# Moving the softmax transposes of the odd attention heads into another pair of PSUM banks

## The chip, the core and the metric

The kernel runs on one core of a Trainium2 chip. The metric is the device time of one execution in microseconds (us). Of TensorE's clock the profile gives the share that was granted; full speed is 2.4 GHz.

The names of the engines in the rows are those of the profile: PE is TensorE's matmul, PEld its weight load, DVE is VectorE, ACT is ScalarE, POOL is GpSimd, SP is the engine whose queue starts the transfers.

## What is computed

Two layers of an encoder over 256 tokens of width 1024. Each layer is a half-step feed-forward block, a mixing block, and another half-step feed-forward block. The mixing block is where the change lies:

```
h = rms_norm(x);  z = h @ w_in            # q, k, v of two attentions, and two gates
o_sw = sliding_window_gqa(...)            # 8 heads of 64, 2 key heads, a learned sink per head
o_na = neighbourhood_attention(...)       # 8 heads of 64
merged = g_A * (o_na @ P_A) + g_B * (o_sw @ P_B);   x = x + merged @ w_out
```

Each attention head computes scores of 256 queries against 256 keys, adds a bias, takes a softmax over the keys and multiplies by the values.

## The kernel before

The 256 tokens are two tiles of 128 rows (T = 2). A float32 matmul is done as three matmuls of split operands (`three`, L166 to L169): every weight piece that arrives by DMA is split into a high part by ACT (L181) and a low part by DVE (L182), and the two parts sit in rings of six (`RING`). PE thus runs a nearly unbroken stream of 512-column matmuls.

The mixing block (`mix`) projects in an order that is written out by hand in the string `ORDER`: Q and K are the queries and keys of the sliding window, q, k, v those of the neighbourhood attention, g the gates. Between the projections, tokens `a4`, `a5` and so on start the next head: first the 8 heads of the sliding window (`sw`), then the 8 of the neighbourhood (`na`). A head passes through three functions, which the kernel puts off by a count of matmuls (`defer`, `tick`, with the lags `P_LAG` and `V_LAG`):

- `front` (L522 to L550): four score matmuls into a PSUM tile `sc` (L536), DVE adds the bias and takes the row extremum (L539), ACT the exponential (L542), DVE the reciprocal of the row sum (L548), POOL scales the rows, which are then the softmax rows `S` (L549).
- `turn` (L553 to L561): PE transposes the 256 x 256 rows in four 128 x 128 pieces into one PSUM bank, the tile `pt` (L557). ACT copies it out as the high part `ph` (L181), DVE then computes the low part `pl` from `pt` and `ph` (L182). The bank is free again when both have read it.
- `back` (L564 to L580): the transposed rows times the values into the PSUM tile `po` (L571), then out by ACT and DVE (L575, L576).

The eight PSUM banks are given out by pools: `ps_g` has two for the projections (tag `g`), `ps_acc` has one for `pt`, one for `po` and two for `sc`, and `ps_tp` has two (tag `tp`) for all other transposes. In the mixing block those are the turns of the queries (L480), the turns of the keys (L497) and the merging of the two branches (L696). A turn of the keys of the neighbourhood uses both `tp` banks at once, four heads in each. ACT copies a bank out as `kh` (L499), and DVE then computes `kl` from the bank and `kh` (L500).

PE's order is the order in which the program issues (it is scheduled by hand); the orders of ACT, DVE and POOL are set when the kernel is built, by a planner that simulates the engines. All three functions of a head have raised priority there.

In the text below, a head is named by its attention and its number from 0: sw h3 is the fourth head of the sliding window. The transposes of the 16 heads of a layer run on PE in the order sw h0 to h7, na h0 to h7.

Of the kernel before, what the change touches and what calls it, by code (L numbers as in the profile page):

```python
# [11 lines left out]
F32 = mybir.dt.float32  # L12
# [9 lines left out]
P = 128  # L22
# [4 lines left out]
T = S // P  # L27
# [28 lines left out]
def hybrid_encoder(ctx, tc, x, w_gu1, w_d1, w_in, b_gate, qk_gain, rpb, sink, t5,  # L56
# [8 lines left out]
    ps_acc = ctx.enter_context(tc.tile_pool(name="ps_acc", bufs=1, space=PSUM))  # L65
    ps_tp = ctx.enter_context(tc.tile_pool(name="ps_tp", bufs=2, space=PSUM))
# [85 lines left out]
    def defer(lag, key, fn):  # L152
        later.append((now[0] + lag, len(later), key, fn))
        later.sort(key=lambda e: e[0])

    def need(*keys):
        for e in [e for e in later if e[2] in keys]:
            later.remove(e)
            e[3]()
# [16 lines left out]
    def flipped(ap):  # L176
        step, n = ap.ap[-1]
        return bass.AP(tensor=ap.tensor, offset=ap.offset + step * (n - 1), ap=[*ap.ap[:-1], [-step, n]])

    def split_to(hi, lo, src):  # L180
        linked("act", lambda: nc.scalar.activation(hi, src, AF.Copy))  # L181
        linked("dve", lambda: nc.vector.tensor_tensor(lo, src, hi.bitcast(F32), ALU.subtract))  # L182
# [272 lines left out]
    def mix(l, n, after):  # L455
        with tc.tile_pool(name="mix", bufs=1) as mp:
# [52 lines left out]
            def attend(name, ins, qT, kh, kl, kidx, bias_of, vcol, ready, oT, sink_l=None):  # L509
                oh, ol = oT  # L510
                po = [None, None]
                with tc.issue_after(rstd_done[0].ins):
                    bias = [bias_of(0), bias_of(1)]

                def urgent(fn):
                    def run(*args):
                        with tc.high_priority(500):
                            fn(*args)
                    return run

                @urgent
                def front(h):  # L522
                    need(*ins)
                    if h + 2 < NH:
                        bias.append(bias_of(h + 2))
                    b = bias.pop(0)
                    least = FMAX
                    if sink_l is not None:
                        sk, least = (v[:, sink_l * NH + h:sink_l * NH + h + 1] for v in (snk, nsnk))
                    ps = ps_acc.tile([P, T, S], F32, name="sc", tag="sc", bufs=2)  # L530
                    S_ = mp.tile([P, T, S], F32, name="S", tag="S", bufs=LAG)
                    mx = small.tile([P, T], F32, name="mx", tag="mx")
                    sm = small.tile([P, T], F32, name="sm", tag="sm")
                    for t in range(T):
                        for i, k in enumerate((kh, kl)):
                            nc.tensor.matmul(ps[:, t, :], qT[:, h, t * P:(t + 1) * P], k[:, kidx(h), :],  # L536
                                             start=i == 0, stop=i == 1)
                    for t in range(T):
                        nc.vector.tensor_tensor_reduce(S_[:, t, :], ps[:, t, :], b(t), -1.0, least,  # L539
                                                       ALU.add, ALU.min, mx[:, t:t + 1])  # L540
                    for t in range(T):
                        nc.scalar.activation(S_[:, t, :], S_[:, t, :], AF.Exp, bias=mx[:, t:t + 1], scale=-1.0,  # L542
                                             accum_out=sm[:, t:t + 1])
                    if sink_l is not None:
                        es = small.tile([P, T], F32, name="es", tag="es")
                        nc.scalar.activation(es, mx, AF.Exp, bias=sk)
                        nc.vector.tensor_tensor(sm, sm, es, ALU.add)
                    nc.vector.reciprocal(sm, sm)  # L548
                    nc.gpsimd.tensor_tensor(S_, S_, sm.unsqueeze(2).to_broadcast([P, T, S]), ALU.mult)  # L549
                    defer(P_LAG, (name, h, 0), lambda: turn(h, S_))  # L550

                @urgent
                def turn(h, S_):  # L553
                    tp = ps_acc.tile([P, T, T, P], F32, name="pt", tag="pt")
                    for t in range(T):
                        for kt in range(T):
                            nc.tensor.transpose(tp[:, kt, t, :], S_[:, t, kt * P:(kt + 1) * P], ident)  # L557
                    ph = mp.tile([P, T, T, P], F32R, name="ph", tag="ph", bufs=2)
                    pl = mp.tile([P, T, T, P], F32R, name="pl", tag="pl", bufs=2)
                    split_to(ph, pl, tp)  # L560
                    defer(V_LAG, (name, h, 1), lambda: back(h, ph, pl))  # L561

                @urgent
                def back(h, ph, pl):  # L564
                    assert ready()
                    if h % 2 == 0:
                        po[0] = ps_acc.tile([P, 2, T, P], F32, name="po", tag="po")
                        po[1] = mp.tile([P, T, P], F32, name="o", tag="o", bufs=2)
                    for kt in range(T):
                        for i, p in enumerate((ph, pl)):  # L570
                            nc.tensor.matmul(po[0][:, h % 2], vcol(kt, h), p[:, kt], start=kt + i == 0,  # L571
                                             stop=kt + i == 2)
                    a, b = (0, DH) if h % 2 == 0 else (DH, 0)
                    o, ov = po[1], flipped(po[0][:, h % 2])
                    nc.scalar.activation(o[a:a + DH], ov[b:b + DH], AF.Copy)  # L575
                    nc.vector.tensor_tensor(o[a:a + DH], o[a:a + DH], ov[a:a + DH], ALU.add)  # L576
                    if h % 2:
                        split_to(oh[:, h // 2], ol[:, h // 2], o)

                for h in range(NH):  # L580
                    yield lambda h=h: front(h)
# [79 lines left out]
            for token in ORDER.split():  # L661
                if token[0] == "a":
                    it, h = next(heads)
# [149 lines left out]
```

## Time and profile before

| | |
|---|---|
| median of 3 runs | 1094.89 us (1094.21 to 1095.57) |
| the profiled execution | 1094.91 us, of it a span of 1093.1 us |
| PE busy | 1079.0 us (99%) |
| DVE busy | 855.3 us (78%) |
| ACT busy | 659.2 us (60%) |
| POOL busy | 116.2 us (11%) |
| granted TensorE clock | 1.000 |

The span goes from the first to the last instruction. PE has matmuls in flight in 99% of it; matmuls overlap in the pipeline, so the start of one against the start of the next says more than the busy time. A 512-column matmul starts some 0.23 us after the one before it, though each is shown as 0.39 us long.

### The profile page before, as it was taken

The numbers are of one execution on the slowest core, as the hardware profiler recorded it, in microseconds if no ns is written. First come the engines' busy times: TensorE is split into PE (matmuls) and PEld (weight loads), VectorE is DVE, ScalarE is ACT, GpSimd is POOL, SyncE is SP. The second block draws the span as 40 slices with busy tenths as digits, with TensorE's granted clock in tenths as the row PEclk, the third lists the DMA queues.
The fourth block names the chain that finished last, engine by engine and source line by source line (L and its number), as shares of the span: only waits on it lengthen the run. The fifth ranks groups of instructions, "written<-read, shape, count | busy, mean of one in ns | idle before, by whom it ended". The sixth has DMA issues, their size and how long they took to land.

```text
span 1093.1 us, 14659 instructions
## 1 busy us (share of the span) xinstructions
PE 1079.0 (99%) x5137; PEld 889.3 (81%) x5137; DVE 855.3 (78%) x1298; ACT 659.2 (60%) x1002; POOL 116.2 (11%) x118
## 2 busy tenths in 40 slices
PE   9999999999999999999999999999999999999998
PEld 7888878888888888887888888788888888888877
DVE  6887778889886778776877786787888767878676
ACT  6665544788764566554465665457877546656442
POOL 1400000243510000000000000003534000000000
PEclk9999999999999999999999999999999999999999
DMA  7876556765654666654757665557666555776553
GB/s 239 267 222 210 185 169 206 232 189 154 192 176 136 209 213 214 210 194 149 245 175 227 215 217 168 189 161 236 185 186 182 177 168 162 226 234 202 183 174 105
DMA packets 98827, 212.62 MB, mean 195 GB/s; under 512 B 7569, under 2 KB 13745, under 8 KB 98753
## 3 DMA queue, kind: packets, MB, share of 16 engines
q1 hardware_dynamic: 98560, 211.60, 61.5%
q8 instruction: 40, 0.66, 0.2%
q0 software_dynamic: 192, 0.08, 0.1%
q14 instruction: 35, 0.28, 0.1%
HBM read 210.59 MB, written 1.06 MB: 194 GB/s over the span
## 4 chain that ended last, share of the span: by engine, by line
PE 78%; DVE 10%; DMA 6%; issue 3%; ACT 3%; DVEq 0%; ACTq 0%
PE g L168 19%; PE g L169 19%; PE g L167 19%; DMA raw<-in_w_d 4%; DVE wl L182 4%; PE acc L167 4%; PE acc L168 4%; PE acc L169 4%; PE tp L314 2%; ACT wh L181 2%; PE tp L198 1%; DVE v L343 1%; PE g L234 1%; PE pt L557 1%; PE sc L536 1%
## 5 line engine op out<-in xcount | busy, mean ns | idle before, releaser
L182 DVE TENSOR_TENSOR wl<-raw,wh 128x1024 fp32r<-128x1024 f32 (+1 forms) x340 | 408.1, 1215 | 66.8 <-ACT wh L181 65.2
L181 ACT ACTIVATE wh<-raw 128x1024 fp32r<-128x1024 f32 (+1 forms) x340 | 349.8, 1045 | 158.6 <-DMA raw<-in_w_d 41.0
L167 PE MATMUL g<-wh,xh 128*128 128x512 f32 (+1 forms) x976 | 389.9, 399 | 0.0
L169 PE MATMUL g<-wh,xl 128*128 128x512 f32 (+1 forms) x976 | 379.0, 388 | 0.0
L168 PE MATMUL g<-wl,xh 128*128 128x512 f32 (+1 forms) x976 | 377.4, 387 | 0.4 <-DVE wl L182 0.4
L169 PEld LDWEIGHTS g<-wh,xl 128*128 128x128 f32 x976 | 183.3, 188 | 40.4 <-DVE xl L182 1.1
L168 PEld LDWEIGHTS g<-wl,xh 128*128 128x128 f32 x976 | 184.0, 189 | 32.1 <-DVE wl L182 0.8
L167 PEld LDWEIGHTS g<-wh,xh 128*128 128x128 f32 x976 | 183.5, 188 | 30.8 <-DVE hh L435 0.2
L433 ACT ACTIVATE sg<-g,rs_y 128x256 f32<-128x256 f32 x88 | 41.5, 471 | 135.3 <-PE g L169 133.8
L343 DVE TENSOR_TENSOR u<-raw 128x512 f32<-128x512 f32 x56 | 38.8, 693 | 79.5 <-DMA raw<-in_w_d 79.2
L167 PE MATMUL acc<-wh,hi 128*128 128x512 f32 x200 | 78.9, 395 | 0.0
L169 PE MATMUL acc<-wh,lo 128*128 128x512 f32 x200 | 78.0, 390 | 0.0
L168 PE MATMUL acc<-wl,hi 128*128 128x512 f32 x200 | 77.9, 389 | 0.0
L173 POOL TENSOR_TENSOR rs_y<-ms,mhalf 128x1 f32<-128x1 f32 x12 | 7.2, 602 | 659.5 <-DVE ms L219 652.5
L435 DVE SCALAR_TENSOR_TENSOR hh<-g,rs_y,sg 128x256 f32<-128x256 f32 x88 | 42.1, 479 | 38.2 <-ACT sg L433 38.0
L549 POOL TENSOR_TENSOR S<-S,sm 128x512 f32<-128x512 f32 x32 | 37.1, 1161 | 71.4 <-DVE sm L548 45.2
L169 PEld LDWEIGHTS acc<-wh,lo 128*128 128x128 f32 x200 | 37.5, 188 | 8.1
L168 PEld LDWEIGHTS acc<-wl,hi 128*128 128x128 f32 x200 | 37.6, 188 | 7.7
L167 PEld LDWEIGHTS acc<-wh,hi 128*128 128x128 f32 x200 | 37.6, 188 | 7.6
L542 ACT ACTIVATE S<-S,mx 128x256 f32<-128x256 f32 x64 | 31.8, 498 | 7.5 <-DVE mx L539 7.4
L314 PEld LDWEIGHTS tp<-ident,hh 128*128 128x128 f32 x176 | 24.5, 140 | 11.7 <-DVE hh L435 0.6
L314 PE MATMUL tp<-ident,hh 128*128 128x128 f32 x176 | 33.4, 272 | 0.0
(190 smaller groups left out, 1460.0 us busy)
## 6 DMA issues: line engine op xcount, KB each, us to landing
raw<-in_w_gu SPq DMA_DIRECT2D x176, 512.0 KB, 4.4
raw<-in_w_d SPq DMA_DIRECT2D x100, 512.0 KB, 4.4
raw<-in_w_in SPq DMA_DIRECT2D x64, 512.0 KB, 4.6
raw<-in_w_out SPq DMA_DIRECT2D x16, 512.0 KB, 3.5
bb<-in_b_gate SPq DMA_DIRECT2D x16, 256.0 KB, 3.7
raw<-in_w_bsw SPq DMA_DIRECT2D x8, 512.0 KB, 4.4
raw<-in_w_bna SPq DMA_DIRECT2D x8, 512.0 KB, 3.5
raw<-in_w_d SPq DMA_DIRECT2D x12, 256.0 KB, 3.6
```

The source lines that it names most:

```text
L167: nc.tensor.matmul(ps, xh, wh, start=first, stop=False)
L168: nc.tensor.matmul(ps, xh, wl, start=False, stop=False)
L169: nc.tensor.matmul(ps, xl, wh, start=False, stop=last)
L181: linked("act", lambda: nc.scalar.activation(hi, src, AF.Copy))
L182: linked("dve", lambda: nc.vector.tensor_tensor(lo, src, hi.bitcast(F32), ALU.subtract))
L198: nc.tensor.transpose(tp[:, i, :], xs[t][:, k * P:(k + 1) * P], ident)
L314: nc.tensor.transpose(tp[:, SLOT[t][i], :], hh[:, i * P:(i + 1) * P], ident)
L343: sub = lambda to, x, y: nc.vector.tensor_tensor(to, x, y, ALU.subtract)
L433: nc.scalar.activation(sg, ps[:, :FC], AF.Silu, scale=rstd[t])
L435: nc.vector.scalar_tensor_tensor(hh, ps[:, FC:], rstd[t], sg, op0=ALU.mult, op1=ALU.mult)
L542: nc.scalar.activation(S_[:, t, :], S_[:, t, :], AF.Exp, bias=mx[:, t:t + 1], scale=-1.0, accum_out=sm[:, t:t + 1])
L549: nc.gpsimd.tensor_tensor(S_, S_, sm.unsqueeze(2).to_broadcast([P, T, S]), ALU.mult)
```

## The change

The transposes of the odd heads take their PSUM tile from the pool `ps_tp`, tag `tp`, in place of `ps_acc`, tag `pt`. Exempt is head 1 of the sliding window (the only attention with `sink_l`), so it is sw h3, h5, h7 and na h1, h3, h5, h7: seven of the sixteen heads of each layer. The other nine stay in the bank `pt`. The sizes, the four transposes of a head and their order on PE, the copies and their engines stay as they are.

```
                 @urgent
                 def turn(h, S_):
-                    tp = ps_acc.tile([P, T, T, P], F32, name="pt", tag="pt")
+                    if h % 2 and (sink_l is None or h > 1):
+                        tp = ps_tp.tile([P, T, T, P], F32, name="pt", tag="tp")
+                    else:
+                        tp = ps_acc.tile([P, T, T, P], F32, name="pt", tag="pt")
                     for t in range(T):
                         for kt in range(T):
                             nc.tensor.transpose(tp[:, kt, t, :], S_[:, t, kt * P:(kt + 1) * P], ident)
```

## Rows read from the trace of the kernel before

**Rows 1.** The page, part 1: busy time of each engine, share of the span, instructions.

```profile
PE 1079.0 (99%) x5137; PEld 889.3 (81%) x5137; DVE 855.3 (78%) x1298; ACT 659.2 (60%) x1002; POOL 116.2 (11%) x118
```

**Rows 2.** Who PE waited for, over the whole span: microseconds in all, times, longest.

```profile
...
PE pt L557 <- DVE sm L548: 2.1, 2, 1.0
PE pt L557 <- DVE pl L182: 1.7, 2, 0.9
...
PE g L168 <- DVE wl L182: 0.4, 1, 0.4
```

**Rows 3.** The timeline of PE in the first layer, around the transposes of sw h3 (256.49) and sw h4 (261.63): start, length, line, what is written from what, count; in brackets the idle time before and what ended it.

```profile
256.25 0.39 PE L169 MATMUL g<-wh,xl 128*128 128x512 f32 x1
256.49 0.60 PE L557 MATMUL pt<-ident,S 128*128 128x128 f32 x4
...
260.39 0.39 PE L169 MATMUL g<-wh,xl 128*128 128x512 f32 x1
261.63 0.63 PE L557 MATMUL pt<-ident,S 128*128 128x128 f32 x4 [0.85 <-DVE pl L182]
```

**Rows 4.** The timeline of DVE there: the low part of sw h2 (253.98), the work up to the two low parts of the keys, the low part of sw h3 (260.81), and the next idle time of DVE.

```profile
253.98 0.68 DVE L182 TENSOR_TENSOR pl<-pt,ph 128x512 fp32r<-128x512 f32 x1
...
256.82 1.21 DVE L182 TENSOR_TENSOR wl<-raw,wh 128x1024 fp32r<-128x1024 f32 x1
257.94 0.75 DVE L500 SCALAR_TENSOR_TENSOR kl<-tp,qkg,kh 128x512 fp32r<-128x512 f32 x1
...
257.94 1.41 DVE L500 SCALAR_TENSOR_TENSOR kl<-tp,qkg,kh 128x512 fp32r<-128x512 f32 x2
...
260.81 0.68 DVE L182 TENSOR_TENSOR pl<-pt,ph 128x512 fp32r<-128x512 f32 x1
...
263.00 0.75 DVE L623 SCALAR_TENSOR_TENSOR gate<-g,rs_y,bb 128x512 f32<-128x512 f32 x1 [0.92 <-PE g L169]
```

**Rows 5.** The last use of the `tp` banks by others before sw h3, on PE and on ACT, and the rows of sw h4 on POOL (timelines of the three engines).

```profile
253.55 1.03 PE L497 MATMUL tp<-ident,kn 128*128 128x128 f32 x8
...
255.87 1.26 ACT L499 ACTIVATE kh<-tp,qkg 128x512 fp32r<-128x512 f32 x2
...
257.08 1.85 POOL L549 TENSOR_TENSOR S<-S,sm 128x512 f32<-128x512 f32 x1 [4.10 <-PE pt L557]
```

**Rows 6.** The timeline of PE in the first layer around the transposes of na h3 (298.95), na h4 (304.50) and na h5 (308.70).

```profile
298.59 0.40 PE L169 MATMUL g<-wh,xl 128*128 128x512 f32 x1
298.95 0.52 PE L557 MATMUL pt<-ident,S 128*128 128x128 f32 x3
...
303.18 0.28 PE L571 MATMUL po<-pl,va 128*128 128x256 f32 x1
304.50 0.52 PE L557 MATMUL pt<-ident,S 128*128 128x128 f32 x3 [1.05 <-DVE sm L548]
...
307.52 0.28 PE L571 MATMUL po<-ph,va 128*128 128x256 f32 x1
...
308.70 0.60 PE L557 MATMUL pt<-ident,S 128*128 128x128 f32 x4
```

**Rows 7.** The timelines of DVE and POOL there: the low parts of na h2 (298.11) and na h3 (303.68), the reciprocal of na h5 (304.28), the output of na h2 (305.47), and the scaled rows of na h4 and na h5.

```profile
298.11 0.69 DVE L182 TENSOR_TENSOR pl<-pt,ph 128x512 fp32r<-128x512 f32 x1
...
303.68 0.68 DVE L182 TENSOR_TENSOR pl<-pt,ph 128x512 fp32r<-128x512 f32 x1
304.28 0.15 DVE L548 RECIPROCAL sm<-sm 128x2 f32<-128x2 f32 x1
...
305.47 0.40 DVE L576 TENSOR_TENSOR o<-o,po 64x256 f32<-64x256 f32 x1
...
297.77 1.04 POOL L549 TENSOR_TENSOR S<-S,sm 128x512 f32<-128x512 f32 x1 [1.39 <-DVE sm L548]
...
304.57 1.88 POOL L549 TENSOR_TENSOR S<-S,sm 128x512 f32<-128x512 f32 x1 [2.89 <-DVE sm L548]
```

**Rows 8.** Busy time of the engines in that stretch, 295 to 307 us (number of instructions in brackets), granted clock, share and rate of the transfers.

```profile
295.00:307.00 12.00, 10.95 (x62) 9.16 (x61) 10.66 (x22) 9.14 (x20) 6.18 (x4) 1.00 0.60 184
```

**Rows 9.** The same places in the second layer: PE at sw h3 (797.58), sw h4 (802.73), na h3 (840.19), na h4 (845.75), and the first low part of the keys on DVE.

```profile
797.58 0.60 PE L557 MATMUL pt<-ident,S 128*128 128x128 f32 x4
...
801.49 0.39 PE L169 MATMUL g<-wh,xl 128*128 128x512 f32 x1
802.73 0.52 PE L557 MATMUL pt<-ident,S 128*128 128x128 f32 x3 [0.85 <-DVE pl L182]
...
839.68 0.40 PE L169 MATMUL g<-wh,xl 128*128 128x512 f32 x1
840.19 0.63 PE L557 MATMUL pt<-ident,S 128*128 128x128 f32 x4
...
844.46 0.28 PE L571 MATMUL po<-pl,va 128*128 128x256 f32 x1
845.75 0.41 PE L557 MATMUL pt<-ident,S 128*128 128x128 f32 x2 [1.01 <-DVE sm L548]
...
799.04 0.74 DVE L500 SCALAR_TENSOR_TENSOR kl<-tp,qkg,kh 128x512 fp32r<-128x512 f32 x1
```

**Rows 10.** Two of the first lines of PE in the kernel (timeline): five matmuls of 512 columns without data, and the first transposes behind them.

```profile
4.66 2.48 PE L117 MATMUL idle<-blank 128*128 128x512 f32 x5
6.94 0.66 PE L198 MATMUL tp<-ident,x 128*128 128x128 f32 x4
```

## The prediction

> **What bounds the kernel now.** The page's busy times come first [rows 1]: PE is busy in 99% of the span, DVE in 78%, ACT in 60%. So only time in which PE stands still can be won, and any new standstill of PE is paid in full. The second view is who PE waited for [rows 2]. The entries for `pt` make 3.8 us in four waits, all in the mixing blocks; a wait for a split weight (`wl`) occurs once, for 0.4 us, so the weights come early enough. The third view is the timeline of PE at those waits, read by starts, since idle time counted from modelled ends comes out too small. A transpose starts 0.24 us after the 512-column matmul ahead of it (256.25 to 256.49) [rows 3]. sw h4 starts at 261.63, where 260.39 + 0.24 = 260.63 was due: 1.00 us lost. na h3: 298.95 against 298.83, 0.12. na h4: 304.50 against 303.18 + 0.12 (a 256-column matmul is half as long) = 303.30, 1.20 [rows 6]. In the second layer the same heads lose 802.73 - 801.73 = 1.00, 840.19 - 839.92 = 0.27 and 845.75 - 844.58 = 1.17 [rows 9]. Together 2.32 + 2.44 = **4.76 us**.
>
> What each waited for shows on DVE: the low part `pl` of the head before. sw h3's ends at 260.81 + 0.68 = 261.49, and sw h4 starts 0.14 later [rows 3, 4]; na h2's ends at 298.80 and na h3 starts 0.15 later; na h3's ends at 304.36 and na h4 starts 0.14 later [rows 6, 7]. The view of waits names a reciprocal (`sm`) for na h4, because one ends at 304.43; but that is na h5's, which na h4 does not read, and the constant 0.14 points to `pl`. So these are waits for the one bank `pt`.
>
> **The change, part by part.** No instruction is added, removed or reordered on PE, no transfer changes, and no queue is moved past. Only the bank that seven heads wait for is another.
>
> *Waits removed.* After the change sw h4 follows sw h2 in `pt`, whose low part ends at 254.66, and its own rows are scaled at 257.08 + 1.85 = 258.93 [rows 4, 5]: nothing holds it at 260.63. na h3 goes to `tp`, which by then only earlier odd heads have used. na h4 follows na h2 (298.80), with its rows scaled at 298.81 [rows 7]. The two waits of that stretch go as well. Gain **4.76 us**, if nothing else is late next.
>
> *A wait added.* The two `tp` banks are not idle when sw h3 comes. PE fills both with the keys of the second token tile at 253.55, 2.94 us ahead of it; ACT reads the first from 255.87 on, and DVE reads it last: `kl` of the first four heads runs 257.94 to 258.69, behind a weight split of 1.21 us [rows 4, 5]. sw h3 starts at 256.49 now; it would have to start at 258.69 + 0.14 = 258.83, **2.34 us later**. In the second layer `kl` ends at 799.78, so 799.92 against 797.58, again 2.34 [rows 9]. All of PE queues behind it: the scores of sw h5, the gate projection, and sw h4. Nothing that decides when `kl` runs comes after sw h3 on PE, so I see no reason for another place of `kl` in DVE's queue.
>
> Bounds of this term, for each layer. Below: if the planner put `kl` right behind its `kh` (first half of 1.26 us, so about 256.50), it would end at 257.25 and leave 257.39 - 256.49 = 0.90; nothing would be left if ACT too took the keys ahead of its weight split. Above: if the bank given is that of the second four heads, whose `kl` ends at 257.94 + 1.41 = 259.35, it is 3.00; with one more split of 1.21 us ahead, 3.55. I take 2.34, the order that the trace shows in both layers.
>
> A page of the Trainium skill, "Perfetto Trace Analysis", section "Optimizing Tensor Performance" (Matmuls), says that independent groups should rotate through different PSUM banks so that the evacuation of one overlaps the next. By that rule alone the 4.76 us would be the result; the rows of the keys say that the other banks are in use at the one place that matters.
>
> *The other odd heads* find `tp` free: sw h5 comes behind sw h4, which is not before 261.63, and the keys' second bank is free at 259.35 [rows 3, 4]; later ones each have a bank of which the head four before was the last user. na h5, at 308.70, needs its rows, scaled at 306.45, 2.25 us early [rows 6, 7].
>
> *What is late next.* After sw h4 PE is 2.34 - 1.00 = 1.34 us behind the trace of before. DVE stands idle for 0.92 us at 263.00 waiting for PE [rows 4], so it can follow. At na h3 and na h4 PE gets 0.12 and 1.20 back and is level again.
>
> *The sum.* First layer 2.34 - 2.32 = +0.02, second 2.34 - 2.44 = -0.10; together **-0.08 us**. The profiled execution took 1094.91 us (span 1093.1 and 1.8 around it), practically the median of 1094.89. Forecast **1094.8 us**: no change. What a measurement of this kernel can tell from no change is some 0.2%, 2.2 us.
>
> **The rivals.**
>
> *A. The keys are out of the way (faster).* The planner, which simulates the banks too, gives `kl` and `kh` earlier places, so that sw h3 does not wait: 1094.91 - 4.76 = 1090.15 us. If only `kl` moves, behind its `kh`, 0.90 us are left in each layer: 1094.91 - 4.76 + 1.80 = 1091.95. For it: both instructions are ready before they run, since the keys' transposes are done 1.3 us ahead of `kh` and a split of 1.21 us runs ahead of `kl` though it is not urgent. Against it: the same order stands in both layers, and nothing ahead of it changes.
>
> *B. The saved waits return at `back` of na h3 (slower).* DVE is busy in 10.66 of the 12 us from 295 to 307 [rows 8]. Without the wait of na h4, PE comes to `back` of na h3 as early as it does now, at 307.52, though all before it ran 1.34 us late [rows 6]. `back` writes the bank that DVE reads for the output of na h2 until 305.87 [rows 7]. With the usual 0.14 us the wait begins once that read ends after 307.38, 1.5 us later than now; a slip of DVE by the whole 1.34 us just does not reach it, so DVE's order would have to get worse too. The price is at most what was saved there, 1.32 and 1.44 us in the two layers: 1094.83 + 2.76 = 1097.6.
>
> *C. The clock falls in the long wait (slower).* The longest idle time of PE behind a first matmul is now 1.05 us [rows 6], and the clock stays granted in full through it (1.00) [rows 8]; 2.34 us are not in the trace. At the start of the kernel, before PE had worked for long, five 512-column matmuls took 6.94 - 4.66 = 2.28 us [rows 10], where later 5 x 0.23 = 1.15 do: the lower of the two levels, 1.2 against 2.4 GHz. One such stretch in each layer adds 2 x 1.13 = 2.3 us: 1097.1 or more.
>
> "TensorE: Matmul & The Clock Gate" in the Trainium skill, Part 1, says that the slow clock is the state at rest and that activity lifts it; no run shown so far has an idle time as long as the one forecast.
>
> **How the numbers follow.** The forecast gets 0.55: all its terms are read at one place and recur in both layers. A gets 0.25, since the order of two instructions decides it. B gets 0.14, C 0.06. The forecast's own range is 1092.9 (a `kl` about 1 us earlier) to 1096.2 (2 x 0.66, the second bank). The range for 8 in 10 reaches down over A to 1090.0 and up to B's price, 1097.6; it leaves out the far end of C, splits that slip twice, and gains above 4.9 us. Faster by over 0.2% is A, 0.25; slower by over 0.2% is B and C, 0.20; within it, 0.55.
>
> **What would show it.** In the changed profile PE should start the transposes of sw h3 some 0.14 us after the first `kl`, with an idle time of about 2 us in front, in both layers, and `tp` or `kl` should appear among what PE waited for. sw h4, na h3 and na h4 should start 0.24 and 0.12 us after the matmul ahead of them; later users of `tp` should show no wait. The forecast is wrong if sw h3 starts without that idle time (A), if `po` shows a wait at na h3 (B), or if matmuls behind sw h3 start 0.45 us apart (C).

## The result, and the profile after

The changed kernel took 1096.95 us in the median (1094.15 to 1098.66 over 20 runs), the kernel before 1094.91 us; the ratio is 1.0019, with a 95% interval of 1.0012 to 1.0025. It is slower by 2.0 us, and its runs spread over 4.5 us (those before over 1.6 us, without one run of 3409.17 us, which the ratio leaves out). The mean granted clock differs from run to run: 0.997 in eight of the 20 runs (1097.8 us on average), 0.998 in nine (1096.7 us), 0.999 or 1.000 in three (1094.8 us); the kernel before has 0.999 or 1.000 in every run of the experiments below. In the profiled run, 1095.51 us with a span of 1093.7 us, it is 0.998.

Who PE waited for in the changed kernel, over the whole span (microseconds, times, longest):

```profile
PE pt L560 <- DVE kl L500: 4.4, 2, 2.2
PE idle L117 <- DVE blank L112: 1.7, 1, 1.7
PE g L168 <- DVE cl L182: 1.6, 4, 0.8
PE tp L198 <- DVE x L299: 1.3, 3, 0.4
PE sc L536 <- DVE skT L500: 0.6, 2, 0.3
PE g L168 <- DVE wl L182: 0.4, 1, 0.4
```

The four waits of `pt` [rows 2] are gone, and two waits for the keys' low part `kl` have come. Rows 2 leave out the largest entry of that view before the change:

```profile
PE g L168 <- DVE cl L182: 2.5, 6, 0.9
```

`cl` is the low part of a weight of the feed-forward blocks; after the change it is 1.6 us in four waits. They lie outside the mixing blocks in both kernels. The other entries stand as they were. (`turn` now has its transposes in line 560, `back` its matmuls in line 574.)

The timeline of PE in the first layer: sw h3 at 258.46, sw h4 at 262.63, na h3 at 299.79, na h4 at 304.15; below it DVE's first `kl`:

```profile
255.87 0.39 PE L169 MATMUL g<-wh,xl 128*128 128x512 f32 x1
258.46 0.63 PE L560 MATMUL pt<-ident,S 128*128 128x128 f32 x4 [2.20 <-DVE kl L500]
...
262.39 0.39 PE L169 MATMUL g<-wh,xl 128*128 128x512 f32 x1
262.63 0.60 PE L560 MATMUL pt<-ident,S 128*128 128x128 f32 x4
...
299.56 0.39 PE L169 MATMUL g<-wh,xl 128*128 128x512 f32 x1
299.79 0.60 PE L560 MATMUL pt<-ident,S 128*128 128x128 f32 x4
...
304.03 0.28 PE L574 MATMUL po<-pl,va 128*128 128x256 f32 x1
304.15 0.60 PE L560 MATMUL pt<-ident,S 128*128 128x128 f32 x4
...
257.56 0.74 DVE L500 SCALAR_TENSOR_TENSOR kl<-tp,qkg,kh 128x512 fp32r<-128x512 f32 x1
```

sw h3 was due at 255.87 + 0.24 = 256.11 and comes at 258.46, 2.35 us late and 0.16 us after `kl` ends at 258.30 (before: no wait [rows 3]). sw h4 follows its matmul by 0.24 us, na h3 by 0.23, na h4 by 0.12: the waits of [rows 3, 6] are gone.

In the second layer the same wait has a sequel. The timeline of PE there, and below it the busy times and the granted clock (the column after POOL) in the stretch behind sw h3 of either layer:

```profile
796.50 0.39 PE L169 MATMUL g<-wh,xl 128*128 128x512 f32 x1
799.09 0.63 PE L560 MATMUL pt<-ident,S 128*128 128x128 f32 x4 [2.20 <-DVE kl L500]
...
800.13 0.63 PE L167 MATMUL g<-wh,xh 128*128 128x512 f32 x1
800.56 0.63 PE L168 MATMUL g<-wl,xh 128*128 128x512 f32 x1
...
803.44 0.40 PE L167 MATMUL g<-wh,xh 128*128 128x512 f32 x1
803.68 0.40 PE L168 MATMUL g<-wl,xh 128*128 128x512 f32 x1
```

```profile
259.00:263.00 4.00, 4.00 (x26) 3.44 (x25) 2.93 (x10) 2.26 (x7) 0.94 (x1) 1.00 0.68 190
799.90:803.30 3.40, 3.40 (x12) 2.82 (x11) 2.26 (x9) 1.79 (x6) 0.46 (x1) 0.50 0.65 199
```

From 799.9 to 803.3 the granted clock is 0.50, so 1.2 in place of 2.4 GHz, and the 512-column matmuls start 0.43 us apart (800.13 to 800.56) in place of 0.23 to 0.24 (803.44 to 803.68). Ahead of that PE had stood idle for 2.20 us. In the first layer of the same execution the same idle time, 2.20 us too, left the clock at 1.00.

How much that is shows in the length of the mixing block, from its first score matmul (first layer 226.41) to its first merge (333.30). Every kernel of this case has those two instructions; the differences of their starts, in us:

| kernel, profiled run | first layer | second layer | clock behind sw h3, first and second layer |
|---|---|---|---|
| before | 106.90 | 107.02 | 1.00, 1.00 |
| changed | 106.89 | 108.47 | 1.00, 0.50 |
| changed, second profile (below) | 108.45 | 108.43 | 0.50, 0.50 |

Where the clock holds, the block takes what it took before, 106.9 us. Where it falls, it takes some 1.56 us more.

### The profile page after: what moved, and what is told of

Read it like the earlier page. It is cut to its first block, busy times and chain, and to the rows that moved or that the text cites. A ratio compares the mean times of both kernels' runs of the same rounds, so it can differ in the third digit from the quotient of the medians.

```text
span 1093.7 us, 14647 instructions
## 1 busy us (share of the span) xinstructions
PE 1079.7 (99%) x5137; PEld 889.7 (81%) x5137; DVE 855.1 (78%) x1298; ACT 659.0 (60%) x1002; POOL 117.5 (11%) x118
```

## The experiments

The theory: the banks do what the forecast says, and the loss comes from the clock, which falls in many executions behind the 2.2 us in which PE stands idle ahead of sw h3. The rivals: the loss is that wait itself, or another order of DVE and ACT in the later heads (the planner did reorder a few instructions behind `kl`: 22 of the 1298 of DVE and 16 of the 1002 of ACT stand elsewhere than before), or time lost outside the mixing block. Expectations are in microseconds of the device. Experiments 1 to 4 shared a chip and 19 runs of the kernel before (median 1094.75), 5 to 7 another one and 29 runs (1095.01). Gains and losses below go by the ratio, which can differ by some tenths of a us from the difference of the medians.

**1. sw h3 back in the old bank.**

```
-                    if h % 2 and (sink_l is None or h > 1):
+                    if h % 2 and (sink_l is None or h > 3):
```

> The change without sw h3: odd heads take the other banks only from sw h5 on. Theory (the added wait of sw h3 and the clock that falls behind it make the loss): no wait for kl, the clock stays at 1.000 in every run, sw h4 waits 1.0 us for the low part of sw h3 again, na h3 and na h4 do not wait; 1094.9 - 2.76 = 1092.1 us. Rival (the loss comes from another order of DVE and ACT in the later heads, or from the clock falling by itself with the other banks): 1095 us or more, clock under 1.000 in some runs.

Measured: 1092.23 us, ratio 0.9974 (0.9963 to 0.9984), which is 2.8 us faster than before (2.5 by the medians); clock 0.999 to 1.000 in all 7 runs. The timeline of PE has sw h4 waiting for the low part again, and nothing else of `pt`:

```profile
260.13 0.39 PE L169 MATMUL g<-wh,xl 128*128 128x512 f32 x1
261.37 0.63 PE L560 MATMUL pt<-ident,S 128*128 128x128 f32 x4 [0.85 <-DVE pl L182]
```

The mixing blocks take 105.50 and 105.49 us, 1.40 and 1.53 less than before; the waits of na h3 and na h4 were read as 1.32 and 1.44. So those gains are kept in full, and the loss hangs on sw h3 alone; whether it is the wait or the clock, this run cannot tell, since both are gone.

**2. sw h3 alone in the other banks.**

```
-                    if h % 2 and (sink_l is None or h > 1):
+                    if sink_l is not None and h == 3:
```

> Only sw h3 takes the other banks, the other six odd heads stay in the old one. Theory: the wait of 2.35 us per layer for kl, 1.00 us per layer given back at sw h4, the waits of na h3 and na h4 as before; 1094.9 + 2.7 = 1097.6 us at full clock and, with the clock falling behind the wait in about 1.2 of the two layers at 1.7 us each, about 1099.6 us, clock 0.997 to 1.000 by run. Rival (the later odd heads make the clock fall, or lose the time): 1097.6 us or less, clock 1.000 in every run.

Measured: 1098.58 us, ratio 1.0039 (1.0026 to 1.0051). Two of the 6 runs had a clock of 1.000 and took 1097.48 and 1098.14 us; the other four, at 0.997 or 0.998, 1097.62 to 1101.62. Expected were 1097.6 at full clock, which came, and 1099.6 in the middle, which lies inside the interval (1.0026 to 1.0051 times 1094.75, 1097.6 to 1100.3) but 1.0 us over the median; the clocks tell of five falls in the 12 waits (by the count that the account of the prediction explains), fewer than the 1.2 a run that were expected. The profiled run has the wait in both layers and the waits of the neighbourhood as before:

```profile
PE pt L560 <- DVE kl L500: 4.4, 2, 2.2
PE pt L560 <- DVE sm L548: 2.1, 2, 1.0
```

One layer of it takes 108.27 us at full clock, 1.37 more than before (2.34 - 1.00 was forecast), the other 109.81 us with the clock at 0.50 from 801.3 to 804.7.

**3 and 6. The wait filled with ten matmuls.** The edit, on top of the change (6 is the same kernel as 3, run again):

```
+                    if sink_l is not None and h == 3:
+                        fill = ps_acc.tile([P, T, S], F32, name="fill", tag="pt")
+                        for _ in range(10):
+                            nc.tensor.matmul(fill, ident_r, qT[:, :T, :], start=True, stop=True)
                     if h % 2 and (sink_l is None or h > 1):
```

> The change whole, and ten 512-column matmuls without use (sqT against the identity, into the bank pt, which is free there) ahead of the transposes of sw h3 on PE: they take about 2.3 us, the time of the wait, so that PE works through it. Theory (the clock falls because PE stands idle): clock 1.000 in every run, hardly any spread, 1095.0 us, 2 us under the change. Rival (the wait as such costs the time, or the order of the other engines does): as the change, about 1097 us with a spread of 4 us. A PE that did not have the time to spare would show it as up to 4.5 us more.

Measured: 1096.27 us, ratio 1.0016 (1.0007 to 1.0024), clock 0.999 to 1.000 in all 12 runs. The clock came out as the theory has it, the time did not: 1095.0 was expected. Nor did the spread: hardly any was expected, and the runs go from 1094.81 to 1098.92 us. Hence the repetition:

> The change with ten matmuls in the wait, once more, as its first median of 1096.3 us left 1.3 us over the forecast open. Theory: clock 1.000 in all runs, 106.9 us from first score matmul to first merge in both layers; what is over 1095.0 us then comes from the feed-forward blocks, which the change does not touch, and scatters as the kernel before does on this chip. Rival (the filled wait costs something in the mixing block): over 107.5 us there.

Measured: 1096.08 us, ratio 1.0008 (0.9999 to 1.0016), clock 0.999 to 1.000 in all 11 runs. The mixing blocks take 106.88 and 106.87 us in the first profile, 106.91 and 106.88 in the second, as before the change. What is too much lies behind: from the second layer's first merge to the last matmul the two profiles have 215.7 and 215.6 us, and 214.1 to 214.4 in every other kernel of this case. It was expected to scatter, and does not: both show it at the same place of the last feed-forward block. Here are PE and DVE in the second profile:

```profile
935.44 0.39 PE L169 MATMUL g<-wh,xl 128*128 128x512 f32 x1
936.84 0.44 PE L314 MATMUL tp<-ident,hh 128*128 128x128 f32 x2 [1.02 <-DVE hh L435]
```

```profile
926.77 0.69 DVE L343 TENSOR_TENSOR u<-raw 128x512 f32<-128x512 f32 x1 [4.97 <-DMA raw<-in_w_d]
...
936.31 0.48 DVE L435 SCALAR_TENSOR_TENSOR hh<-g,rs_y,sg 128x256 f32<-128x256 f32 x1
```

And DVE in the changed kernel:

```profile
925.99 0.69 DVE L343 TENSOR_TENSOR u<-raw 128x512 f32<-128x512 f32 x1 [3.59 <-DMA raw<-in_w_d]
```

PE wants the activation `hh`, and DVE is late with it, because it had waited longer for a weight of `in_w_d` some 10 us earlier. Counted from the second layer's first merge (874.90 in the second profile, 875.49 in the changed kernel), DVE starts on that weight at 51.9 us (first profile: 51.7), and at 50.2 to 50.7 in every other kernel; it does not catch up before `hh`. The orders of DVE, ACT, POOL and SP are those of the changed kernel. Why this weight lands later with ten matmuls and not with five (experiment 7) was not tried; the lateness lies behind both mixing blocks, and these take what they took before the change.

**5. The change again, beside the filled variants.** No edit.

> The change itself, beside the filled variants on the same chip. Theory (idle PE in the wait of sw h3 makes the clock fall, in each layer by itself): clock 0.997 to 0.998 in most runs, about 1.0 to 1.7 us for each fall, 1096.9 us in the middle; the mixing block takes 106.9 us from its first score matmul to its first merge where the clock holds, and 108.5 us where it falls. Rival: the loss lies outside the mixing block, and that stretch takes 106.9 us in both layers.

Measured: 1097.57 us, ratio 1.0021 (1.0008 to 1.0034); clock 0.997 in seven of the 12 runs (1097.9 us on average), 0.998 in three (1095.6), 0.999 in one (1093.7), 0.995 in one (1102.9; no profile tells why this one is so low and so slow). Its profiled run has the clock low in both layers:

```profile
258.70:262.10 3.40, 3.40 (x13) 2.92 (x12) 2.50 (x9) 1.87 (x6) 0.00 (x0) 0.50 0.62 192
801.40:804.80 3.40, 3.40 (x13) 2.91 (x12) 2.54 (x9) 1.88 (x6) 0.00 (x0) 0.50 0.60 191
```

Both mixing blocks take 108.4 us. The rival, a loss outside the mixing block, falls. The order of DVE, ACT and POOL is the same in this run and in experiment 7, instruction by instruction.

**7. The wait half filled.** As 3, with `range(5)`.

> Five matmuls in the wait in place of ten: 1.2 us of idle time are left ahead of sw h3, close to the 1.05 us through which the kernel before kept its clock. Theory (the length of the idle time decides): clock 1.000 in every run, time as with ten, about 1095 us. Rival (the clock falls by the bank or by the place, however long PE idles): 0.997 to 0.998 in most runs and about 1097 us.

Measured: 1094.84 us, ratio 1.0000 (0.9991 to 1.0009), clock 0.999 to 1.000 in all 12 runs. PE and DVE in the first layer, and the busy times and the granted clock behind sw h3 in both layers:

```profile
256.55 1.33 PE L557 MATMUL fill<-sqT,ident_r 128*128 128x512 f32 x5
258.91 0.63 PE L564 MATMUL pt<-ident,S 128*128 128x128 f32 x4 [1.02 <-DVE kl L500]
...
258.01 0.75 DVE L500 SCALAR_TENSOR_TENSOR kl<-tp,qkg,kh 128x512 fp32r<-128x512 f32 x1
```

```profile
259.00:263.00 4.00, 4.00 (x24) 3.53 (x25) 3.39 (x11) 2.26 (x7) 0.48 (x1) 1.00 0.66 212
800.00:804.00 4.00, 4.00 (x25) 3.44 (x24) 3.10 (x11) 2.26 (x7) 0.77 (x1) 1.00 0.63 191
```

1.02 us of idle time are left, about as long as the longest in the kernel before (1.05) [rows 6], and the clock holds. The mixing blocks take 106.89 and 106.84 us. On the same chip the unfilled change has 1.0021. Between the two kernels PE's stop for `kl` is the same, since sw h3 starts 0.15 to 0.16 us after `kl` in both; only what PE does in it differs, the order of the other engines being the same. So the loss against the kernel before is the clock's; the wait itself is still paid, and it uses up what the removed waits give back.

**4. The even heads in place of the odd ones.** The rows point to this version: sw h4 finds the other banks free, and if it moves, sw h3 can stay.

```
-                    if h % 2 and (sink_l is None or h > 1):
+                    if h % 2 == 0 and (sink_l is None or h > 3):
```

> The even heads from sw h4 on take the other banks, the odd heads and the first four stay: sw h4 is the first in tp, 2 us after the keys' first bank is free. Theory: none of the six waits of the kernel before is left and none is added; 1094.9 - 4.76 = 1090.1 us, clock 1.000 in every run, no wait of pt in the view of waits. Rival (waits taken away there come back at the next input that DVE is late with): 1092 us or more with waits at po or sc.

Measured: 1089.87 us (1089.53 to 1090.45), ratio 0.9956 (0.9944 to 0.9968), 4.8 us faster than before (4.9 by the medians); clock 0.999 to 1.000 in all 5 runs. The transposes of sw h3, h4 and h5 on PE:

```profile
256.66 0.60 PE L560 MATMUL pt<-ident,S 128*128 128x128 f32 x4
260.80 0.60 PE L560 MATMUL pt<-ident,S 128*128 128x128 f32 x4
266.36 0.60 PE L560 MATMUL pt<-ident,S 128*128 128x128 f32 x4
```

None has idle time ahead of it, and no wait of `pt` is left in the view of waits. The mixing blocks take 104.50 and 104.54 us; the forecast's 2.32 and 2.44 us off the kernel before are 104.58 and 104.58.

## Why the prediction was wrong

**What bounds the kernel, and the waits removed: right.** All six waits for the one bank `pt` go, and what they cost is what was read from starts: 4.76 us, measured as 4.8 where nothing takes their place (experiment 4). That the reciprocal named by the view of waits was not the cause also holds: with na h3 in another bank na h4 starts at 304.15, 0.12 us after its matmul, and the reciprocal runs only behind that:

```profile
305.24 0.15 DVE L548 RECIPROCAL sm<-sm 128x2 f32<-128x2 f32 x1
```

The prediction's "so the weights come early enough" overlooks the waits for `cl`, 2.5 us in all; as they lie outside the mixing block, they change nothing in the sum.

**The wait added: right.** 2.34 us were forecast for sw h3 in each layer, 2.35 were found, behind the `kl` of the first four heads, in the place of DVE's queue where the kernel before has it.

**What is late next: right.** PE was level again behind na h4, and DVE followed; `back` of na h3 shows no wait (rival B did not come).

**The sum: the step that failed.** It took -0.08 us as the whole result, and so counted the added wait at its length, with nothing for the clock. The wait also has the price of rival C: the clock falls behind it to half for 3.4 us and costs about 1.56 us each time (108.47, 108.45 or 108.43 us against 106.89 for the block). One fall lowers the mean clock of a run by 0.5 x 3.4 / 1094 = 0.0016. Read by that, 0.998 is one fall and 0.997 two, as in the profiled runs of the change (0.998 with one, 0.997 with two); 0.999 and 1.000 also occur in the kernel before and count as none. So the 20 runs have two falls in eight, one in nine, none in three: an estimated 25 falls in 40 waits. 25 x 1.56 / 20 = 1.95 us per run, close to the loss of 2.0 us. Experiment 5 can be read in the same way: its clocks make 20 falls (three in the run with 0.995, one more than it has such waits), 20 x 1.56 / 12 = 2.6 us, and it lost 2.6 us by the medians. The forecast of -0.08 us is what the change takes when the clock is kept, by five matmuls in the wait (1.0000) or by chance (three runs at 1094.8 us on average).

That 1096.95 us lies inside the range of 8 in 10 is luck: the range goes so high for the price of rival B, which did not come, while the forecast's own range ends at 1096.2. Rival C's 1097.1 us is close by luck too: it has two falls in each run at 1.13 us, and measured are some 1.25 falls at 1.56 us. And the 0.2% that the text takes for the least that can be told was too coarse: the interval tells 1.0019 from no change.

Rival C was named, with its place and its sign, and 0.06 as its chance. That was too little on what the text itself said: the longest idle time through which the trace showed the clock holding was 1.05 us, and 2.3 us were to come. Its price per layer was set at 1.13 us or more, from five matmuls at the start; measured are 1.56. The page named there, "TensorE: Matmul & The Clock Gate" of the Trainium skill, Part 1, gives the lower clock as that of an idle TensorE, and the trace agrees that idle time can bring it back. How much of it that takes is told here by the runs alone: 2.2 us did it in some 25 of 40 waits, by the count above, and 1.0 us in none. Where between the two it begins was not tried.

**Rival A** (the keys out of the way) did not come: DVE's order up to `kl` is that of before; the instructions that moved come behind it.

## What to carry to other kernels

Before an alternation between buffers is laid over a pool that others use, find the last reader of that pool at the first place where the new user comes: here shifting the alternation by one head turned a loss of 2.0 us into a gain of 4.8 us. A new wait of TensorE that is longer than any through which the trace shows its clock holding can have a second price, the work behind it at half the clock. The spread of the runs does not tell of it: experiment 3 spreads over 4.1 us at 0.999 to 1.000, and the kernel before over 4.9 us beside experiments 5 to 7. The mean granted clock does: it is worth reading in each run to the third digit, since one fall in this kernel of 1.1 ms is 0.0016.

## What the runs showed of the hardware that was not expected

The same idle time, 2.20 us, at the same place of the program let the clock fall in one layer and not in the other of one execution; what decides it is not shown. A short use of PE without purpose was worth its time: five 512-column matmuls, 1.2 us of an idle 2.35, kept the clock at 0.999 to 1.000 in all 12 runs.
